# When a paced background step may run: tying the sample-memory sets of a hybrid decoder kernel to the rounds that close a weight group

## The chip, the cores and the metric

The kernel runs on one core of a Trainium2 chip. The metric is the device time of one execution in microseconds. Three executions of the kernel before took 2805.95, 2803.56 and 2801.19 us; their median is 2803.56 us.

## The reference: one step of a two-layer recurrent decoder

The model has 288 tokens: a prompt of 256 and 8 samples of 4 tokens each. Its width is 2048. Layer 0 mixes with a diagonal state space and gated linear attention, layer 1 with an mLSTM of 4 heads of size 512; behind each comes an RMS norm and a squared-ReLU MLP of width 8192. Everything is float32. For this case the mLSTM of layer 1 matters. Each sample brings, for each head, a memory matrix C of 512 x 512 that is both read and updated:

```
num   = (q k^T * w) v + wp * (q C)
den   = sum(q k^T * w) + wp * (q n)
h     = num / max(|den|, exp(-m))
C_new = decay * C + sum_s wk_s k_s v_s^T
```

The 8 samples times 4 heads make 32 matrices of 1 MB, which are loaded, multiplied by the queries, scaled, added to and written back.

## The kernel before, in words

**The stream.** All big products are one stream on TensorE. A `Group` is a weight slice of up to 256 columns; its rows are worked off in *rounds* of 512 rows (four tiles of 128, two column blocks). A round (`mm`, L212) multiplies each of the 8 weight tiles three times against 288 columns, high and low parts of weights and activations (L222, L223, L224), so 24 matmuls. Weights of 2048 rows take 4 rounds, of 1024 rows 2 rounds. The first round of a group *opens* it and takes two PSUM tiles `g` from a pool of two (`psg`, L97); the last *closes* it, and `mm` then emits the evacuations of both tiles (L225 to L228), one VectorE multiplication of 128x288 each: `mq_evac` L1393, `mk_evac` L1396, `mv_evac` L1401, `mo_evac` L1418. While layer 1 runs, `three` is False (L1287), so the next group needs the same two tiles: its opening round waits for the two evacuations.

**Weights.** `load` (L183, SyncE queue) and `cast` (L192) run ahead. A cast makes `wh` on ScalarE (L200) and `wl` on VectorE (L201), two of each per round. The cast that is emitted behind the matmuls of round i is for round i+2.

**The paced steps.** Beside the stream there are generators, kept in `side`. After each round `run` (L230) calls `pump` (L136), with one credit for a full round. Each generator gets its rate times that and makes one step for each whole credit. Steps of `ml_head` (L1423) and `ml_fin` (L1599) have rate 1.0. `ml_mem` (L1546) has rate 0.32 (`R_MEM`, L24), is the only one with `late=1`, and so comes last in the pump. A step may also wait for a flag, and then uses its credit up without work (`until`, L132). `finish` (L153) forces the steps of a generator when a `need` falls due.

**One set of the memories** is one step of `ml_mem`, for two of the eight times 512 KB of a head's samples in a quarter of its rows: 4 matmuls that read the memory into `n` (L1577, two passes each, so x8 in the trace), 4 matmuls of 32 rows that make the new outer products `pb` (L1582, first into the one tile of `psx`, then into three tiles of `pss`, a pool of 3 that every paced step shares), and 4 VectorE operations of 128x512 that scale and add (L1586). After the second and the fourth of them GpSimd's queue issues a store of the tile (L1588) and the load of the tile that comes six half sets later (L1561) into the same buffer; the load waits for the store. There are 8 sets a head, 32 in all. `mem{h}` is set behind the eighth.

**Other paced steps** that the text names: in `ml_head` the scores (L1453), the transposes of k (L1462), a block of small VectorE operations (L1468 to L1481, called the qp block here), the products L1484 and L1492 with a VectorE operation that frees the PSUM tile of the latter (L1494), the denominators with a reciprocal (L1507 to L1514), L1517, four steps with L1528 and four with L1538, whose PSUM tile ScalarE copies out (L1540). In `ml_fin`: L1608, a multiplication of 128x1152 (L1615), squares, and the RMS norm (L1628), which calls `rms` (L288): a square root on ScalarE (L291) and a reciprocal on VectorE (L292).

**Rounds of layer 1** are numbered here from 1, the first of q of head 0. Each of q, k, v and the output gate takes 8 rounds a head, in the order q0 k0 v0, q1 k1 v1, o0, q2 k2 v2, q3 k3 v3, o1, o2, o3; rounds 129 to 160 are the output projection, with a closing round every second one. Up to 128 every fourth closes.

The credits, as the kernel before has them:

```python
for s in sorted(self.side, key=lambda s: s[4]):
    s[2] += s[1] * part
    while s[2] >= 1.0:
        s[2] -= 1.0
        if not self.step(s):
            break
```

Of the kernel before, what the change touches and what calls it, by code (L numbers as in the profile page):

```python
# [21 lines left out]
EPS = 1e-6  # L22
NEG = -1e30
R_S5, R_GLA, R_ML, R_MEM = (1.0, 1.2, 1.15), 1.0, 1.0, 0.32  # L24
R_GST, R_DEC, N_U = 0.5, 0.6, 2


_CONST = {}
# [58 lines left out]
class Base:  # L87
# [45 lines left out]
        while name not in self.flags:  # L133
            yield

    def pump(self, part):  # L136
        for s in sorted(self.side, key=lambda s: s[4]):
            s[2] += s[1] * part
            while s[2] >= 1.0:
                s[2] -= 1.0  # L140
                if not self.step(s):
                    break
# [28 lines left out]
    def flush(self, all_=False):  # L171
        again = True
        while again:
            run, keep = [], []
            for e in self.later:
                e[0] -= 1
                (run if all_ or e[0] <= 0 else keep).append(e)
            self.later = keep
            for e in run:
                e[1]()  # L180
            again = all_ and bool(self.later)
# [48 lines left out]
    def run(self, ahead_load=3, ahead_cast=1):  # L230
        seq = []
        for it in self.items:
            if isinstance(it, Group):
                seq.extend(dict(g=it, k0=k0, n=min(KG, it.nk - k0)) for k0 in it.order)
            else:
                seq.append(it)
        grs = [s for s in seq if isinstance(s, dict)]
        nl = nq = i = 0
        for s in seq:
            if not isinstance(s, dict):  # L240
                s()
                continue
            while nl < min(len(grs), i + ahead_load + 1):
                if nl < len(self.pre):
                    self.pre[nl][0]()
                self.load(grs[nl])
                nl += 1
            while nq < min(len(grs), i + ahead_cast + 1):
                if nq < len(self.pre):
                    self.pre[nq][1]()  # L250
                self.cast(grs[nq])
                nq += 1
            self.mm(s)
            part = 0.5 * s["g"].nm
            s.clear()
            if nq < min(len(grs), i + ahead_cast + 2):
                if nq < len(self.pre):
                    self.pre[nq][1]()
                self.cast(grs[nq])
                nq += 1  # L260
            self.flush()
            self.pump(part)
            i += 1
        self.flush(all_=True)
        self.finish()
# [1000 lines left out]
class Layer1:  # L1266
# [156 lines left out]
    def ml_head(self, h):  # L1423
# [42 lines left out]
        s = self.smp[h] = {}  # L1466
# [42 lines left out]
        nc.tensor.matmul(ps[:, TP:T], lhsT=on[0:32], rhs=w[0:32, 384:416], start=True, stop=False)  # L1509
        nc.tensor.matmul(ps[:, TP:T], lhsT=on, rhs=qn[:, 0, :], start=False, stop=True)  # L1510
        rec = s["rec"] = p.tile([128, T], F32, name="rec", bufs=2)
        act.activation(out=rec, in_=ps, func=AF.Abs)
        v.tensor_max(out=rec, in0=rec, in1=em)
        v.reciprocal(out=rec, in_=rec)  # L1514
# [84 lines left out]
    def ml_fin(self, h):  # L1599
        nc = self.nc  # L1600
        v, act = nc.vector, nc.scalar
        p = self.mlh
        yield from self.until(f"mem{h}")
        yield
        s, hn = self.smp[h], self.hn[h]
        ps = self.pss.tile([128, 4, NS], F32, name="s")
        for e in range(4):
            nc.tensor.matmul(ps[:, e, :], lhsT=s["o"][:, e * 128:e * 128 + 128], rhs=self.c("sel"), start=True, stop=True)  # L1608
        t = p.tile([128, 4, NS], F32, name="inter")
        v.tensor_tensor(out=t, in0=ps, op=ALU.mult,  # L1610
                        in1=s["rec"][:, TP:T].rearrange("p (o t) -> p o t", o=1).to_broadcast([128, 4, NS]))
        v.tensor_add(out=hn[:, :, TP:T], in0=hn[:, :, TP:T], in1=t)
        self.flags.add(f"num{h}")
        yield from self.until(f"so{h}")
        v.tensor_mul(out=hn, in0=hn, in1=self.so[h])  # L1615
        yield
        acc = p.tile([128, T], F32, name="facc")
        for e in range(4):
            if e == 0:
                act.activation(out=acc, in_=hn[:, 0, :], func=AF.Square)  # L1620
            else:
                sq = self.tmp.tile([128, T], F32, name="sq")
                act.activation(out=sq, in_=hn[:, e, :], func=AF.Square)
                v.tensor_add(out=acc, in0=acc, in1=sq)
        yield
        yield
        ps = self.pss.tile([128, T], F32, name="s")
        nc.tensor.matmul(ps, lhsT=self.ones, rhs=acc, start=True, stop=True)  # L1628
        self.rms(acc, ps, 512)
        yield  # L1630
        if h >= 2:
            q, ns = ((self.mlp1, ("q1", "k1")), (p, ("hn", "so")))[h - 2]
            yh, yl = (q.tile([128, 4, T], F32R, name=n, **({} if h == 2 else dict(bufs=2))) for n in ns)
        else:
            yh, yl = (p.tile([128, 4, T], F32R, name=n, bufs=2) for n in ("yh", "yl"))
        self.yy[h] = (yh, yl)
        for e in range(4):
            t = hn[:, e, :]
            v.scalar_tensor_tensor(out=t, in0=t, scalar=self.ml_nw[:, e:e + 1], in1=acc, op0=ALU.mult, op1=ALU.mult)
        yield  # L1640
        for e in (0, 2):
            es = slice(e, e + 2)
            act.activation(out=yh[:, es], in_=hn[:, es], func=AF.Copy)
            self.defer(lambda es=es: v.tensor_tensor(out=yl[:, es], in0=hn[:, es], in1=yh[:, es].bitcast(F32),
                                                     op=ALU.subtract), 0)
            if e == 0:
                yield
        self.flush()
        self.flags.add(f"y{h}")
# [255 lines left out]
```

## Time and profile before

| | before |
|---|---|
| median of 3 executions | 2803.56 us |
| the profiled execution | 2805.46 us |
| its span | 2803.70 us |
| TensorE matmuls busy | 2770.3 us (99%) |
| TensorE weight loads busy | 2679.4 us (96%) |
| VectorE busy | 1704.9 us (61%) |
| ScalarE busy | 1347.2 us (48%) |
| GpSimd busy | 212.5 us (8%) |
| mean granted TensorE clock | 0.996 of full speed |

Layer 1 lies between about 1300 and 1990 us of the span, the memory sets between 1414 and 1882 us. Shares of busy time are averages; a matmul's duration in the trace (about 296 ns for 288 columns) is longer than the distance from one to the next, so TensorE's waits are to be read from starts and from the waits that the profile names. A row of a timeline gives start, duration, engine, line, operation, output<-inputs, shapes and count, and in brackets the idle time before it and what ended it; for x3 the duration covers the three.

### The profile page before, as it was taken

How to read it: one execution, taken by the hardware profiler on the slowest of the kernel's cores; microseconds unless marked ns; L12 is line 12 of the kernel's file. 1: busy time of each engine (PE TensorE's matmuls, PEld its weight loads, DVE VectorE, ACT ScalarE, POOL GpSimd, SP SyncE). 2: the span in 40 equal slices, each digit the busy share in tenths (PEclk: the TensorE clock that was granted, in tenths of full speed). 3: DMA queues.
4: the chain of work that ended last, by engine and by line, in shares of the span. 5: the costliest groups of instructions: out<-in, count | busy, mean ns of one | idle time of the engine just before them, and what ended most of it. 6: DMA issues, size and time to landing. Idle time of an engine off the chain costs nothing. (4 is left out here: it accounts for less than half of the span.)

```text
span 2803.7 us, 52666 instructions
## 1 busy us (share of the span) xinstructions
PE 2770.3 (99%) x20688; PEld 2679.4 (96%) x20688; DVE 1704.9 (61%) x3235; ACT 1347.2 (48%) x2464; POOL 212.5 (8%) x327
## 2 busy tenths in 40 slices
PE   9999999999999999999999999999999999999999
PEld 8988999999999999999988888889999999999999
DVE  7887668555555555557456655777555555555555
ACT  5646755544444444445434343445544444444445
POOL 3110111000000000000112222210000000000000
PEclk9999999999999999999999999999999999999999
DMA  7454567555555555555678878885555555555554
GB/s 212 129 155 140 162 194 227 163 166 166 162 169 165 164 164 165 162 167 150 194 233 262 277 240 277 263 262 160 164 165 165 166 166 166 162 169 161 168 164 136
DMA packets 449737, 511.94 MB, mean 183 GB/s; under 512 B 23315, under 2 KB 423405, under 8 KB 449457
## 3 DMA queue, kind: packets, MB, share of 16 engines
q1 hardware_dynamic: 414320, 412.67, 48.9%
q0 software_dynamic: 28176, 90.22, 10.2%
q10 hardware_dynamic: 6992, 5.68, 0.6%
q8 instruction: 163, 2.67, 0.4%
q14 instruction: 86, 0.70, 0.1%
HBM read 460.15 MB, written 47.56 MB: 181 GB/s over the span
## 5 line engine op out<-in xcount | busy, mean ns | idle before, releaser
L200 ACT ACTIVATE wh<-raw 128x512 fp32r<-128x512 f32 x1556 | 963.1, 629 | 1211.1 <-PE g L223 875.7
L201 DVE TENSOR_TENSOR wl<-raw,wh 128x512 fp32r<-128x512 f32 x1556 | 1036.3, 688 | 663.7 <-ACT wh L200 647.9
L222 PE MATMUL g<-xh,wh 128*128 128x288 f32 x2936 | 885.9, 302 | 6.7 <-DVE so L1418 3.0
L224 PE MATMUL g<-xh,wl 128*128 128x288 f32 x2936 | 867.0, 295 | 3.0 <-DVE wl L201 2.9
L223 PE MATMUL g<-xl,wh 128*128 128x288 f32 x2936 | 869.3, 296 | 0.0
L222 PEld LDWEIGHTS g<-xh,wh 128*128 128x128 f32 x2936 | 553.5, 189 | 22.8 <-issue 12.8
L224 PEld LDWEIGHTS g<-xh,wl 128*128 128x128 f32 x2936 | 555.5, 189 | 4.4 <-DVE wl L201 4.4
L223 PEld LDWEIGHTS g<-xl,wh 128*128 128x128 f32 x2936 | 554.4, 189 | 2.6 <-issue 2.4
L223 PE MATMUL g<-hl,wh 128*128 128x288 f32 x1352 | 400.2, 296 | 0.0
L224 PE MATMUL g<-hh,wl 128*128 128x288 f32 x1352 | 399.5, 296 | 0.0
L222 PE MATMUL g<-hh,wh 128*128 128x288 f32 x1352 | 399.2, 295 | 0.0
L222 PE MATMUL x<-xh,wh 128*128 128x288 f32 x920 | 274.2, 298 | 0.0
L224 PE MATMUL x<-xh,wl 128*128 128x288 f32 x920 | 271.3, 295 | 1.1 <-DVE wl L201 1.1
L223 PE MATMUL x<-xl,wh 128*128 128x288 f32 x920 | 272.0, 296 | 0.0
L222 PEld LDWEIGHTS g<-hh,wh 128*128 128x128 f32 x1352 | 256.9, 190 | 0.0
L224 PEld LDWEIGHTS g<-hh,wl 128*128 128x128 f32 x1352 | 253.5, 188 | 0.0
L223 PEld LDWEIGHTS g<-hl,wh 128*128 128x128 f32 x1352 | 253.3, 187 | 0.0
L223 PE MATMUL x<-hl,wh 128*128 128x288 f32 x696 | 206.0, 296 | 0.0
L224 PE MATMUL x<-hh,wl 128*128 128x288 f32 x696 | 205.7, 296 | 0.0
L222 PE MATMUL x<-hh,wh 128*128 128x288 f32 x696 | 205.5, 295 | 0.0
L224 PEld LDWEIGHTS x<-xh,wl 128*128 128x128 f32 x920 | 173.8, 189 | 1.3 <-DVE wl L201 1.3
L222 PEld LDWEIGHTS x<-xh,wh 128*128 128x128 f32 x920 | 173.1, 188 | 0.9 <-issue 0.8
(567 smaller groups left out, 2949.6 us busy)
## 6 DMA issues: line engine op xcount, KB each, us to landing
raw<-in_w_mlp_up_dram SPq DMA_DIRECT2D x256, 512.0 KB, 3.7
raw<-in_w_mlp_down_dram SPq DMA_DIRECT2D x256, 512.0 KB, 3.6
raw<-in_w_in_odd_dram SPq DMA_DIRECT2D x128, 512.0 KB, 4.6
raw<-in_w_in_even_dram SPq DMA_DIRECT2D x64, 512.0 KB, 4.0
cin<-in_state_mlstm_c_dram POOLq DMA_DIRECT2D x64, 512.0 KB, 5.5
out_sample_mlstm_c_dram<-cin POOLq DMA_DIRECT2D x64, 512.0 KB, 6.0
raw<-in_w_out_even_dram SPq DMA_DIRECT2D x32, 512.0 KB, 4.3
raw<-in_w_out_odd_dram SPq DMA_DIRECT2D x32, 512.0 KB, 3.6
```

What stands on the lines that cost most here:

```text
L200: nc.scalar.activation(out=wh[:, 0:n], in_=src, func=AF.Copy)
L201: nc.vector.tensor_tensor(out=wl[:, 0:n], in0=src, in1=wh[:, 0:n].bitcast(F32), op=ALU.subtract)
L222: nc.tensor.matmul(g.ps[j], lhsT=wh, rhs=xh, start=opens and k == 0, stop=False)
L223: nc.tensor.matmul(g.ps[j], lhsT=wh, rhs=xl, start=False, stop=False)
L224: nc.tensor.matmul(g.ps[j], lhsT=wl, rhs=xh, start=False, stop=closes and k == n - 1)
```

## The change

`pump` gets a second argument, whether the round just done closed its group. A generator with `late` set keeps its credit, without a step, while that credit is under `LATE` = 1.8 and either the round did not close a group or one of three marked steps ran in this pump: the denominators (L1511), the 128x1152 multiplication (L1615) and the RMS norm of a head (L1629). From 1.8 on it steps in any round, once for each whole credit. Nothing else is touched: the same instructions are issued, in another order.

```diff
-R_GST, R_DEC, N_U = 0.5, 0.6, 2
+R_GST, R_DEC, N_U, LATE = 0.5, 0.6, 2, 1.8
...
-    def pump(self, part):
+    def pump(self, part, closes):
+        self.busy = False
         for s in sorted(self.side, key=lambda s: s[4]):
             s[2] += s[1] * part
+            if s[4] and s[2] < LATE and (self.busy or not closes):
+                continue
             while s[2] >= 1.0:
                 s[2] -= 1.0
                 if not self.step(s):
...
-            part = 0.5 * s["g"].nm
+            part, closes = 0.5 * s["g"].nm, s["g"].ps is None
             s.clear()
...
-            self.pump(part)
+            self.pump(part, closes)
...
         rec = s["rec"] = p.tile([128, T], F32, name="rec", bufs=2)
+        self.busy = True
         act.activation(out=rec, in_=ps, func=AF.Abs)
...
         v.tensor_mul(out=hn, in0=hn, in1=self.so[h])
+        self.busy = True
         yield
...
         self.rms(acc, ps, 512)
+        self.busy = True
         yield
```

## Rows read from the trace of the kernel before

**Rows 1.** Busy time by stretch (us, busy and count of each engine, PEclk, DMA, GB/s).
```profile
1200.00:1300.00 100.00, 100.00 (x752) 100.00 (x751) 65.87 (x124) 50.30 (x93) 0.00 (x0) 1.00 0.55 164
1500.00:1600.00 100.00, 97.52 (x694) 82.49 (x694) 66.51 (x107) 40.61 (x70) 25.36 (x40) 1.00 0.87 270
```

**Rows 2.** Waits of TensorE from 1310 to 1900 us: total us, times, longest.
```profile
PE g L222 <- DVE so L1418: 3.0, 2, 1.5
PE s L1582 <- ACT sq L291: 1.2, 1, 1.2
```

**Rows 3.** Timeline of TensorE and VectorE, rounds 63 to 65.
```profile
1574.92 1.07 PE L1577 MATMUL n<-cin,qp 128*32 128x512 f32 x8
1576.35 0.40 PE L222 MATMUL g<-xh,wh 128*128 128x288 f32 x1
1578.22 2.06 DVE L1586 SCALAR_TENSOR_TENSOR cin<-cin,wps,s 128x512 f32<-128x512 f32 x3
1580.20 0.82 DVE L1393 TENSOR_TENSOR q<-g,rbc 128x288 f32<-128x288 f32 x2
1580.79 0.37 PE L222 MATMUL g<-xh,wh 128*128 128x288 f32 x1 [0.98 <-DVE q L1393]
```

**Rows 4.** Timeline of VectorE and TensorE, rounds 51 to 53.
```profile
1516.22 1.95 DVE L1514 RECIPROCAL rec<-rec 128x288 f32<-128x288 f32 x1
...
1521.80 0.40 PE L222 MATMUL g<-xh,wh 128*128 128x288 f32 x1 [1.50 <-DVE so L1418]
```

**Rows 5.** Timeline of TensorE, rounds 125 to 127: L1538 alone, then with a set.
```profile
1847.71 1.88 PE L1538 MATMUL s<-vt,kw 128*128 128x512 f32 x4
1849.02 0.70 PE L222 MATMUL g<-xh,wh 128*128 128x288 f32 x1
...
1852.62 1.88 PE L1538 MATMUL s<-vt,kw 128*128 128x512 f32 x4
1856.20 0.40 PE L222 MATMUL g<-xh,wh 128*128 128x288 f32 x1
```

**Rows 6.** Timeline of TensorE and VectorE, end of round 60.
```profile
1565.13 0.40 PE L222 MATMUL g<-xh,wh 128*128 128x288 f32 x1
1566.24 2.06 DVE L1586 SCALAR_TENSOR_TENSOR cin<-cin,wps,s 128x512 f32<-128x512 f32 x3
```

**Rows 7.** Timeline of TensorE and VectorE, end of round 88.
```profile
1681.97 0.40 PE L222 MATMUL g<-xh,wh 128*128 128x288 f32 x1
1682.55 2.06 DVE L1586 SCALAR_TENSOR_TENSOR cin<-cin,wps,s 128x512 f32<-128x512 f32 x3
```

**Rows 8.** Timeline of TensorE and VectorE, end of round 116.
```profile
1806.53 0.50 PE L1582 MATMUL s<-vs,ks 32*128 32x512 f32 x1 [1.16 <-ACT sq L291]
1806.96 0.40 PE L222 MATMUL g<-xh,wh 128*128 128x288 f32 x1
1809.61 1.40 DVE L1586 SCALAR_TENSOR_TENSOR cin<-cin,wps,s 128x512 f32<-128x512 f32 x2
```

**Rows 9.** Timeline of VectorE and TensorE, rounds 47 and 48.
```profile
1499.70 0.68 DVE L1481 TENSOR_TENSOR hl<-vt,hl 32x512 fp32r<-32x512 f32 x1
1501.15 1.28 DVE L201 TENSOR_TENSOR wl<-raw,wh 128x512 fp32r<-128x512 f32 x2
1502.35 0.34 DVE L1494 SCALAR_TENSOR_TENSOR n<-n,dec,s 128x128 f32<-128x128 f32 x1
1503.22 0.40 PE L222 MATMUL g<-xh,wh 128*128 128x288 f32 x1
```

**Rows 10.** Busy time by stretch, early in layer 1 (columns as in rows 1).
```profile
1329.00:1332.00 3.00, 1.21 (x11) 0.81 (x10) 2.40 (x15) 1.56 (x5) 1.12 (x2) 1.00 0.46 126
1332.00:1335.70 3.70, 3.70 (x17) 3.70 (x18) 1.83 (x8) 0.85 (x2) 0.51 (x2) 0.54 0.83 104
```

**Rows 11.** GpSimd's queue, and the weight loads that waited for a memory tile.
```profile
1861.76 0.71 POOL L1561 DMA_DIRECT2D cin<-in_state_mlstm_c_dram  x1 [7.03 <-DMA out_sample_mlstm_c_dram<-cin]
...
PEld n L1577 <- DMA cin<-in_state_mlstm_c_dram: 1.1, 3, 0.8
```

## The prediction

> **What bounds the kernel now.** I first read busy time by stretch. In a plain stretch TensorE runs without a gap, 752 matmuls in 100 us, so one each 0.133 us and a round of 24 in 3.2 us; in a stretch with memory sets it is still busy for 97.5 of 100 us, VectorE for 66.5 [rows 1]. So TensorE sets the time, and a change of order can only move its waits. Second, TensorE's own waits over the stage of the memories: the largest are two for VectorE before an opening round, 1.5 us each (the output gate's evacuation), and a third of 0.98 us (q's); a further 1.2 us is a wait inside a set for a square root [rows 2, 3]. Third, timelines around these waits, to see what is late and why; last, GpSimd's queue, which feeds the sets.
>
> In the timeline of rounds 63 to 65 a set runs behind round 63, and round 64 closes a group. A set alone holds the stream for 1576.35 - 1574.92 = 1.43 us; its four updates keep VectorE until 1580.28, the two evacuations come behind them, and the opening round 65 starts 0.98 us late [rows 3]. Around round 51 a reciprocal of 1.95 us stands in front of the updates as well, and the wait is 1.50 us [rows 4]; the same happens once more near 1773 us [rows 2].
>
> How good is 97.5% busy as a measure of what can be won? The waits just named, all that have to do with a set, come to 5.2 us. The Trainium skill (Perfetto Trace Analysis, Identifying the Most-Contended Engine) holds that matmul busy time misleads and that the share of weight loading tells the headroom; by it the stretch at 1500 us has 17.5 us in 100 to give, some 80 us over the stage by my estimate. The trace does not agree here: the missing weight loading is time in which matmuls of 512 columns stream behind one small load (the reads of a set [rows 3]). I go by the waits.
>
> **Where the sets go.** Both orders follow from the credits: 0.32 a round from round 17 on, a step for each 1.0, waiting steps counted too. Before, sets run behind rounds 29, 32, 35, 38, 41, 45, 48, 51; 54, 57, 60, 63, 66, 70, 73, 76; 85, 88, 91, 95, 98, 101, 104, 107; 110, 113, 116, 120, 123, 126, 129, 132. With the change I work out: 31, 32, 36, 40, 44, 47, 48, 52; 56, 60, 60, 64, 68, 72, 75, 76; 88, 88, 92, 96, 100, 103, 104, 108; 112, 116, 116, 120, 125, 128, 130, 132. Of 32 sets 27 then stand in a closing round, against 9. But four rounds bring 1.28 credits, more than one set, so the surplus reaches 1.8 five times in another round (31, 47, 75, 103, 125) and reaches 2.0 in three closing rounds (60: 1.76 + 0.32 = 2.08; 88: 2.04; 116: 2.00), where two sets run at once. In 60 and 116 the RMS norm runs too, and the credit overrides the mark. Each head's last set moves by one round at most, and no forced step arises, so the tail of layer 1 stays.
>
> **What is removed.** (1) The 1.5 us wait behind round 51 and its twin behind 107: the sets go to 52 and 108, behind the evacuations in VectorE's order, with three rounds before the next. Minus 3.0 us [rows 2, 4]. (2) The 0.98 us before round 65, as the set of 63 goes to 64: minus 1.0 us [rows 3]. What could be late there next is the weight cast behind the set, but it is due two rounds, 6.4 us, later and the updates take 2.7 us; cost nothing. Without this cover it would cost one cast, 0.64 us [rows 9]. (3) A set in one pump with a product L1538 waits for ScalarE's copy of a PSUM tile: 1856.20 - 1852.62 = 3.58 us, against 1.31 for L1538 alone plus 1.43 for a set, so 0.84 too much [rows 3, 5]. Six sets stand so before (35, 57, 60, 91, 123, 126) and four after (36, the first of 60, 92, 125; the second of 60 is priced below). Two fewer: minus 1.7 us, bounds 0 and minus 1.7.
>
> **What is added.** (4) The two-set rounds. The second set's four products need the four PSUM tiles of the first, so the last of them waits for the first set's last update, and the stream resumes about 0.5 us later (0.43 from the last product to the stream, plus a start [rows 8]). In round 88 the updates end at 1682.55 + 2.06 = 1684.61, the stream resumes at 1685.1 instead of 1681.97 [rows 7]: 3.1 us for 1.43 of work, so 1.7 lost. In round 60 they end at 1568.30, resume at 1568.8 instead of 1565.13 [rows 6]: 3.7 - 1.43 = 2.2 lost. In round 116 the square root already holds the first set for 1.16 us and the reciprocal holds its updates until 1811.01; resume at 1811.5 instead of 1806.96 [rows 8]: 4.55 - 1.43 = 3.1 lost. Together plus 7.0 us; bounds plus 4 (if VectorE gets to the first updates a third earlier) and plus 8. (5) Rounds 47 and 48, twice (103 and 104). The set of 47 stands behind the qp block, which ends at 1500.38. Its four updates (2.7 us) end at 1503.1, then come the evacuations of 48 (0.8), two casts (1.28) and L1494 (0.34), at 1505.5; L1494 frees the PSUM tile that the last product of 48's set needs, so the stream resumes at 1506.0. Without a wait it would at 1503.22 + 1.5 for the set that came in = 1504.7 [rows 9]. So 1.3 us each, plus 2.6; bounds 0 (another free tile) and plus 4. (6) Sets in other pairs (31 with 32, 75 with 76, 125): their updates end before the next closing round's second evacuation is needed, since that round's paced step adds 1 to 3 us of TensorE work. Nothing taken, bounds minus 0.5 and plus 1.5, the size of the wait of [rows 4].
>
> **Queues passed.** Of a moved set its stores and loads on GpSimd's queue move too. There a load waits up to 7.0 us for the store of its buffer [rows 11], two halves a set, some 14 us against 14.6 us between sets on average. So this queue is nearly full, and only the six buffers, three sets of lead, keep the waits for a tile at 1.1 us in three [rows 11]. After the change the tightest place is round 76: its tiles are loaded behind the sets of 60, 60, 64 and 68, four times 14 us behind the first updates at 1566, so by 1622; the set runs 16 rounds behind 1565, 51 us of stream and some 14 of paced steps, near 1630. That leaves 8 us for the load to land. I take nothing; bounds 0 and plus 3. SyncE's weight loads are not passed: they are issued by round, as before.
>
> **The sum.** -3.0 - 1.0 - 1.7 + 7.0 + 2.6 = +3.9 us. The profiled execution took 2805.46 us (span 2803.70 and 1.76 around it), so it would take 2809.4; it lies 1.9 above the median of the three, 2803.56, and against that the forecast is 2807.5 us. That is 0.14%, under the 0.2% (5.6 us) that a measurement of this kernel can tell from no change.
>
> **Rivals.** *The clock falls in the two-set rounds* (slower). Early in layer 1 TensorE did 1.2 us of work in 3 us, waiting for gates, and the next 3.7 us ran at a granted clock of 0.54, the level of 1.2 GHz: 17 matmuls where 28 fit, 1.5 us lost [rows 10]. In round 116 after the change the engine waits for about 4 us with little between. If the clock falls behind all three, it is 3.9 + 3 x 1.5 = 8.4: 2812 us. Against it: the stretch at 1500 us holds a wait of 1.50 and one of 0.98 us at a granted clock of 1.00 [rows 1, 3, 4]. [...]
>
> *The bunched sets drain the buffers* (slower): the second set of a pair waits for its tiles, from the point where the 8 us are used up; half of a load's wait of 7.0 us more [rows 11], 2811 us. For it speaks the queue that is nearly full, against it the lead.
>
> *The second set's waits lie beside work that the stream had to wait for anyway* (faster): then terms 4 and 5 fall to nothing and the removed waits stay, -5.7: 2797.9 us. The waits of [rows 2] speak for it; against it stands the pool of three PSUM tiles.
>
> *The change doesn't do what it says*: if the surplus credit broke the rule most of the time, nothing would move and it would stay at 2803.6; counting gives 27 of 32, so I give it no chance of its own.
>
> **How the numbers follow.** The sum's case has 0.60, the clock 0.14, the buffers 0.11, the faster rival 0.15. The sum's own bounds (-5.7 + 4 + 0 to -4 + 8 + 4) reach from about 2802 to 2812; of its 0.60 I put 0.12 above 5.6 us. The clock and the buffers lie above it whole. The faster rival lies on the edge, so half of it counts. So slower 0.37, faster 0.08, same 0.55. The range of 2799.5 to 2812.5 takes in the sum's bounds, the buffers, the clock at two of three places (2810.5) and the weaker half of the faster rival.
>
> **What would show it.** Right: the waits of q and the output gate on VectorE gone from TensorE's list; in their place waits of L1582 on VectorE's updates (or their PSUM tiles) in rounds 60, 88 and 116 of 2 to 4 us, and on L1494 in 48 and 104 of 1.3 us; granted clock 1.00 in these rounds. Wrong: a second set that follows the first at 1.43 us; waits of L1577 on a load; a stretch at 0.5 of the clock; or new waits before opening rounds.

## The result, and the profile after

The changed kernel is slower by 0.7%: 2825.31 us, median of 6 runs (2818.97 to 2828.17), against 2803.24 (2801.19 to 2807.06, 6 runs) for the kernel before beside it. The ratio is 1.0074 [1.0063, 1.0085]. The forecast was 2807.5 with a range up to 2812.5.

| | before | after |
|---|---|---|
| profiled execution, us | 2805.46 | 2828.17 |
| its span, us | 2803.70 | 2826.40 |
| granted clock, mean | 0.996 | 0.991 |
| matmuls | 20688 | 20688 |

**By stretch.** Lines below the diff have moved by 3 to 6: L222 is now L225, L1538 L1542, L1540 L1544, L1582 L1586, L1586 L1590. The first view is busy time by stretch, with the columns of [rows 1]; its second line answers to the second of [rows 1].

```profile
1400.00:1500.00 100.00, 96.54 (x653) 84.04 (x656) 51.10 (x84) 33.53 (x60) 16.41 (x25) 0.97 0.73 219
1500.00:1600.00 100.00, 97.47 (x656) 81.50 (x649) 64.52 (x106) 39.30 (x69) 22.47 (x34) 0.97 0.79 244
1700.00:1800.00 100.00, 95.95 (x676) 82.90 (x675) 55.71 (x94) 38.70 (x70) 25.38 (x40) 0.97 0.84 255
1800.00:1900.00 100.00, 97.62 (x650) 81.98 (x648) 68.31 (x110) 44.27 (x75) 19.13 (x27) 0.97 0.82 272
```

In the stretch at 1500 us TensorE's busy share is what it was (97.47 against 97.52), yet 656 matmuls ran instead of 694, and the granted clock is 0.97 instead of 1.00. Busy time hides this loss: at half the clock matmuls start 0.24 us apart instead of 0.133, and the engine counts as busy all the same. The two half-clock stretches in this window (at 1528 and 1576 us, below) account for some 22 of the 38 missing matmuls by my estimate; waits, and the other rounds that the window holds, make up the rest.

**TensorE's waits**, 1300 to 1930 us: engine, tile and line that waits, what it waits for; total us, times, longest. They answer to [rows 2].

```profile
PE s L1586 <- ACT cp L1544: 5.9, 3, 3.5
PE s L1586 <- ACT vs L1522: 2.6, 2, 1.3
PE x L1586 <- DVE cin L1590: 1.4, 2, 1.1
PE g L225 <- DVE hr L1713: 1.3, 2, 1.1
PE s L1586 <- ACT sq L294: 1.2, 1, 1.2
PE s L1586 <- DVE n L1497: 0.8, 2, 0.4
```

The waits for `so` (3.0 us) are gone, and so is the one for q. The two largest now are waits of a set's products L1586 for ScalarE: for `cp`, the copy of L1542's result, which the forecast had at 0.84 us a place and shrinking, and for `vs`, which it hadn't at all.

**The clock.** Busy time around three of the places where it fell, and around two where it didn't, round 7 (the place of [rows 10]) and round 88; columns as above.

```profile
1328.00:1331.00 3.00, 1.19 (x11) 0.79 (x10) 2.40 (x15) 1.58 (x5) 1.14 (x3) 1.00 0.48 125
1331.00:1334.70 3.70, 3.70 (x29) 3.70 (x30) 2.18 (x9) 1.28 (x3) 0.49 (x1) 1.00 0.75 109
...
1446.00:1453.50 7.50, 4.04 (x18) 1.22 (x16) 3.72 (x6) 1.57 (x3) 0.70 (x1) 0.94 0.77 240
1453.50:1457.50 4.00, 4.00 (x17) 4.00 (x18) 1.13 (x2) 0.63 (x1) 3.19 (x7) 0.50 0.81 258
...
1523.00:1527.20 4.20, 2.90 (x18) 1.08 (x17) 4.03 (x8) 3.75 (x6) 1.45 (x2) 1.00 0.64 189
1527.20:1531.00 3.80, 3.80 (x18) 3.80 (x19) 2.21 (x4) 0.63 (x1) 0.72 (x2) 0.56 0.96 273
...
1687.00:1693.50 6.50, 6.17 (x38) 2.96 (x36) 5.27 (x9) 0.63 (x1) 0.76 (x1) 1.00 0.46 140
1693.50:1697.00 3.50, 3.50 (x26) 3.44 (x26) 2.81 (x5) 0.81 (x2) 1.43 (x2) 1.00 0.43 129
...
1819.00:1828.00 9.00, 6.78 (x33) 2.75 (x32) 6.70 (x9) 3.08 (x5) 2.71 (x4) 0.81 0.85 270
1828.00:1832.00 4.00, 4.00 (x18) 3.77 (x18) 2.10 (x5) 0.63 (x1) 0.12 (x1) 0.57 0.86 262
```

Behind round 36 (TensorE busy for 4.04 of 7.50 us) the next 4 us hold 17 matmuls at 0.50, the level of 1.2 GHz, where 30 fit, as in [rows 10]. Behind round 52 (2.90 of 4.20 us busy) and round 116 (6.78 of 9.00) it fell as well. In round 88 the engine was busy for 6.17 of 6.50 us and the clock held. Round 7 isn't touched by the change: with the same work, 11 matmuls in 3 us, the clock fell behind it in the profile before (17 matmuls in 3.7 us) and held in the profile after (29). So the same wait costs the clock in one execution and not in another.

**The whole difference, in two sums.** In the timeline of TensorE a round's last stream matmul and the next round's first stand 0.133 us apart where nothing lies between. What lies there beyond 0.133 is the end of a round: the set, the paced step, and their waits. From 1290 to 1940 us, the stage of the memories, the ends add up to 143.92 us before and 160.17 after: plus 16.25. Inside the rounds, matmuls start 0.24 us apart at half the clock instead of 0.133; that costs 1.49 us before, in the one place of [rows 10], and 9.67 after, in six places (2.46 at 1454 us, 1.50 at 1528, 1.46 at 1576, 1.50 at 1719, 1.49 at 1791, 1.26 at 1829): plus 8.2. The wait of q before round 65, behind a round without a step, took 1.14 us from start to start and is gone. Together 16.25 + 8.2 - 1.1 = +23.3 us; the spans differ by 22.7, and layer 1 begins 1.0 us earlier in the profile after.

Ends of the rounds that differ by more than the place of a plain set, us (* a set, ** two; plain L1542 is 1.31, a plain set 1.43 to 1.53):

| round | before | after | | round | before | after |
|---|---|---|---|---|---|---|
| 35, 36 | 3.44*, 1.32 | 1.32, **7.48*** | | 91, 92 | 3.47*, 1.31 | 1.32, **6.06*** |
| 48 | 2.88* | 3.83* | | 104 | 2.89* | 3.83* |
| 51, 52 | 2.85*, 2.09 | 1.32, **3.75*** | | 107, 108 | 2.85*, 2.09 | 1.32, **3.74*** |
| 57, 60 | 3.25*, 3.88* | 1.32, **7.52**** | | 116 | 3.66* | **8.48**** |
| 76 | 1.96* | 2.82* | | 123, 125, 126 | 3.25*, 1.31, 3.59* | 1.31, **3.89***, 1.31 |
| 88 | 2.70* | **5.81**** | | | | |

### The profile page after: what moved, and what is told of

The parts are those of the page before. It is cut to its first block, busy times and chain, and to the rows that moved or that the text cites. A ratio compares the mean times of both kernels' runs of the same rounds, so it can differ in the third digit from the quotient of the medians.

```text
span 2826.4 us, 52666 instructions
## 1 busy us (share of the span) xinstructions
PE 2786.4 (99%) x20688; PEld 2691.1 (95%) x20688; DVE 1705.5 (60%) x3235; ACT 1346.6 (48%) x2464; POOL 212.5 (8%) x327
## 5 line engine op out<-in xcount | busy, mean ns | idle before, releaser
L225 PE MATMUL g<-xh,wh 128*128 128x288 f32 x2936 | 889.6, 303 | 2.7 <-DVE gy L971 1.4
L225 PEld LDWEIGHTS g<-xh,wh 128*128 128x128 f32 x2936 | 556.9, 190 | 17.8 <-issue 12.4
L225 PE MATMUL g<-hh,wh 128*128 128x288 f32 x1352 | 399.2, 295 | 0.0
L225 PE MATMUL x<-xh,wh 128*128 128x288 f32 x920 | 274.2, 298 | 0.0
L225 PEld LDWEIGHTS g<-hh,wh 128*128 128x128 f32 x1352 | 256.9, 190 | 0.0
L225 PE MATMUL x<-hh,wh 128*128 128x288 f32 x696 | 205.5, 295 | 0.0
L225 PEld LDWEIGHTS x<-xh,wh 128*128 128x128 f32 x920 | 173.0, 188 | 0.9 <-issue 0.8
```

What stands on the lines that cost most here:

```text
L225: nc.tensor.matmul(g.ps[j], lhsT=wh, rhs=xh, start=opens and k == 0, stop=False)
```

## The experiments

My theory after the two traces (L): sets wait for PSUM tiles that other work frees late, the copy of L1542's result and the copy L1518 (now L1522) above all, the two-set rounds add theirs, and the clock falls behind these waits. Its rivals: the clock alone is the loss, so that mending one wait only moves the fall; or GpSimd's queue (Q), which can't follow the bunched sets, holds them whatever else is mended. L+Q is both.

Each kernel ran beside the kernel before, whose medians on the three occasions were 2804.15 (15 runs; 1 to 3), 2806.29 (17; `a_fill`, `n_busy`, `a_all`, `n_busy_fix`) and 2804.20 (19; the rest). Times of different occasions are compared by their ratios to it; 0.001 is 2.8 us.

**1 to 3: one suspect at a time.** First round 36 in the kernel after: timeline of TensorE and ScalarE, start and duration in us, then in brackets the idle time before and what ended it.

```profile
1445.36 0.34 ACTq L1545 DMA_DIRECT2D out_prompt_mlstm_c_dram<-cp  x1
1445.93 1.88 PE L1542 MATMUL s<-vt,kw 128*128 128x512 f32 x4
1447.74 1.06 PE L1581 MATMUL n<-cin,qp 128*32 128x512 f32 x8
1452.04 0.60 ACT L1544 ACTIVATE cp<-s 128x512 f32<-128x512 f32 x1 [5.07 <-DMA out_prompt_mlstm_c_dram<-cp]
1452.69 0.79 PE L1586 MATMUL s<-vs,ks 32*128 32x512 f32 x1 [3.46 <-ACT cp L1544]
```

L1542's result was ready near 1447.8. The copy to `cp` started at 1452.04, because `cp` has one buffer and the store of the copy before, issued at 1445.36, had not landed. The copy frees the PSUM tile that the set's last product needs. Copies fall behind at L1542 after L1542: behind rounds 33 to 36 the first waited only for its product, the next three for a store, for 1.83, 3.02 and 5.07 us. Round 36 has the head's fourth.

Then round 52, the same view; it answers to [rows 4]:

```profile
1523.41 0.50 PE L1521 MATMUL s<-hl,rsel 64*128 64x512 f32 x1
1524.04 1.28 ACT L1422 ACT_TABLE_LOAD   x1
1525.33 0.78 ACT L1422 ACTIVATE so<-so 128x288 f32<-128x288 f32 x2
1526.01 0.58 ACT L1522 ACTIVATE vs<-s 128x512 fp32r<-128x512 f32 x1
1526.64 0.50 PE L1586 MATMUL s<-vs,ks 32*128 32x512 f32 x1 [1.30 <-ACT vs L1522]
```

The sigmoids' table load, 1.28 us, stands ahead of the copy L1522 on ScalarE, and the set waits for the PSUM tile that this copy frees.

`a_cp2`, two buffers for the copy (the second in the room of a tile that another one can share):

```diff
-            cp = p.tile([128, 512], F32, name="cp")
+            cp = p.tile([128, 512], F32, name="cp", bufs=2)
...
-        t = p.tile([128, 4, NS], F32, name="inter")
+        t = p.tile([128, 4, NS], F32, name="qn")
```

> The changed kernel with two buffers for the copy of the L1538 product (its small inter tile shares a buffer with qn to make room). Theory L (late tiles): a set that shares a pump with another paced step waits for a PSUM tile that ScalarE or VectorE frees late, and a TensorE kept this thin falls to half clock for a while. In rounds 36 and 92 the copy waits for the store of the copy before. With two buffers the ends of rounds 36 and 92 take 2.7 to 3.5 us instead of 7.5 and 6.1, and the stretches at half clock behind them (2.5 and 1.5 us lost) are gone: 10 to 12 us less than the changed kernel, 2813 to 2815 us. Rival Q (queue): the stores and loads of the sets on GpSimd's queue set the pace now, as their share of the chain of waits suggests; then no tile of ScalarE matters and it stays at 2825 (2822 to 2828).

Measured: 2817.92 us (2813.40 to 2822.93), 1.0052 [1.0037, 1.0066]. Some 6 us less than the kernel after by the ratios, where 10 to 12 were expected. Round 36 fell from 7.48 to 3.25 us, 92 from 6.06 to 3.24, and the clock held behind both. But round 76 grew from 2.82 to 5.73. In the kernel after, this round's last memory tile was already late: the weight load that needs it waited 0.73 us, until 1637.63. Now the round was 7.9 us earlier and the tile only 5.0, so the wait grew to 3.63 us, until 1632.60. The weight loads' waits for memory tiles in that profile:

```profile
PEld n L1581 <- DMA cin<-in_state_mlstm_c_dram: 4.4, 2, 3.6
```

So the copy was the cause of 36 and 92, and behind it stood the rival of the drained buffers, in part. `b_cp2`, the same edit to the kernel before, is the control:

> Control: the kernel before with the same two buffers for the copy. It has no set beside the fourth L1538 of a head but six beside an earlier one, 0.8 us too long at most. Theory L: 0 to 4 us less than before, 2799 to 2803, and no other granted clock. Rival Q: no change, 2803. If it gained as much as the change loses (10 us or more), the copy's buffer would be a bound of its own and not one that the change brings.

Measured: 2802.25 us (11 runs), 0.9991 [0.9982, 1.0000]. The buffer wins next to nothing where no set stands behind four products L1542 in a row.

`a_so2`, the sigmoids one round later:

```diff
-            self.defer(lambda: nc.scalar.activation(out=t, in_=t, func=AF.Sigmoid))
+            self.defer(lambda: nc.scalar.activation(out=t, in_=t, func=AF.Sigmoid), 2)
```

> The changed kernel with the sigmoids of the output gate put off by one more round, so that they and their table load no longer stand ahead of the copy that frees L1521's PSUM tile in rounds 52 and 108. Theory L: the ends of these rounds take about 2.0 us instead of 3.75 and the half clock behind them (1.5 us each) is gone: 6 to 7 us less, 2818 to 2820 us. Rival Q: no change, 2822 to 2828.

Measured: 2824.32 us (2819.95 to 2826.25), 1.0076 [1.0062, 1.0089]. In its profile, rounds 52 and 108 fell from 3.75 to 1.96 us and the clock holds behind them, as expected; it fell at 1452, 1687 and 1818 us instead. The mechanism is confirmed in the two rounds; the gain of 6 to 7 us is not seen in the times. The profile can't say where it went: it is of the fastest of the five executions (2819.95 us), 8.2 us shorter than that of the kernel after, with ends of rounds that add up to 4.6 us less. In the other four executions the granted clock was 0.991 or 0.992, as low as in most of the kernel after, so the clock's part of the gain didn't come; what took the rest stays open, and the intervals leave room for some 4 us.

`a_one`, one set at a time:

```diff
-                if not self.step(s):
+                if not self.step(s) or s[4]:
                     break
```

> The changed kernel with at most one set a pump: the second sets of rounds 60, 88 and 116 run behind 63, 91 and 119. Theory L: the ends of the three rounds go from 7.5, 5.8 and 8.5 us to about 3.9, 2.7 and 3.7, the sets cost 1.4 to 2.2 us where they go to, and the half clock behind 60 and 116 (1.5 and 1.3 us) is gone: 7 to 10 us less, 2815 to 2818 us. Rival Q: the same number of sets in the same time through the same queue, no change, 2822 to 2828.

Measured: 2816.77 us (2811.93 to 2823.22), 1.0049 [1.0033, 1.0065], as expected. The surplus sets went to rounds 63, 91 and 119, at ends of 1.53, 3.31 and 3.86 us.

**4: the clock by itself.** `a_fill` adds 113 matmuls on the stream's own tiles, whose result nothing uses, between the reads and the products of the sets that waited. Nothing that a set waits for comes sooner by them; they only keep TensorE at work meanwhile.

```diff
+                fill = {(0, 2): 26, (2, 2): 17, (0, 7): 10, (2, 7): 10, (1, 2): 14, (2, 1): 14, (3, 1): 8, (3, 2): 14}
+                for _ in range(fill.get((h, n), 0)):
+                    nc.tensor.matmul(pb[0][:, 0:T], lhsT=self.xh[:, 0, 0:128], rhs=self.xh[:, 0, :], start=True, stop=True)
```

> The changed kernel with useless matmuls (128x288, into the tile that the first product of the set overwrites) in the places where a set waits: 26 in round 36, 17 in 92, 10 each in 52 and 108, 14 each in the second sets of 60, 88 and 116, 8 in the first of 116; 113 in all, 15 us of TensorE work at 0.133 us each. Theory C (clock): the six stretches at half clock of the changed kernel's profile (9.7 us lost) come from TensorE standing nearly still in these waits. Filled, the waits are as long as before and the granted clock stays at 1.00: 5 to 9 us less than the changed kernel, 2816 to 2820 us. Rival W (waits alone): the clock has another cause; the filler gains nothing and costs what doesn't fit into the waits, 2825 to 2835 us.

Measured: 2821.79 us (2821.05 to 2823.51), 1.0052 [1.0040, 1.0065]: by the ratios some 6 us less than the kernel after (1.0074 [1.0063, 1.0085]), though the intervals just touch, with 113 x 0.133 = 15 us more matmul work. That is within the 5 to 9 us of theory C; its 2816 to 2820 us are missed only because the kernel before took 3 us longer on this occasion. Busy time around rounds 36, 60 and behind 116 in its profile, the copy of round 36, and TensorE in round 60 (L1586 is the filler here, L1589 the products):

```profile
1445.00:1452.80 7.80, 7.80 (x48) 5.21 (x47) 2.57 (x5) 1.23 (x2) 0.70 (x1) 1.00 0.82 263
1452.80:1457.00 4.20, 4.20 (x34) 4.20 (x33) 3.11 (x5) 1.26 (x2) 3.56 (x7) 1.00 0.77 241
1560.00:1574.00 14.00, 11.76 (x54) 6.57 (x52) 6.41 (x9) 4.13 (x6) 2.83 (x4) 0.77 0.61 191
1828.00:1832.00 4.00, 4.00 (x33) 4.00 (x32) 3.01 (x6) 2.42 (x4) 0.62 (x1) 1.00 0.92 341
```
```profile
1451.00 0.60 ACT L1544 ACTIVATE cp<-s 128x512 f32<-128x512 f32 x1 [5.37 <-DMA out_prompt_mlstm_c_dram<-cp]
...
1567.64 0.79 PE L1589 MATMUL s<-vs,ks 32*128 32x512 f32 x1 [2.12 <-ACT cp L1544]
1568.35 1.94 PE L1581 MATMUL n<-cin,qp 128*32 128x512 f32 x8
1570.22 3.73 PE L1586 MATMUL x<-xh 128*128 128x288 f32 x14
```

The copy waits for its store as before (5.37 us), yet the stream behind round 36 runs at 1.00, 34 matmuls in 4.2 us, and in the stage of the memories no stretch of the stream is at half clock. Only in round 60 did the clock fall, and there the filler bears the theory out in its own way: it stood only before the second set's products, but in this execution the first set waited 2.12 us for ScalarE's copy with nothing to fill it. Behind that wait the second set's eight reads took 1.94 us instead of 1.06 and the 14 fillers 3.73 instead of 1.9, and the round grew to 13.38 us. So the ends of the rounds take 4.5 us more than in the kernel after, and the stream between them gives back 9.9. The half clock is thus a consequence of the thin waits, and its cost is apart from theirs. The executions agree: their mean granted clock is 0.995 to 0.996, against 0.991 to 0.994 for the kernel after, and they lie within 2.5 us against 9.2.

**5: which part of the rule.** `n_busy` keeps the marks and drops the closing round; `c_only` does the reverse.

```diff
-            if s[4] and s[2] < LATE and (self.busy or not closes):
+            if s[4] and s[2] < LATE and self.busy:
```

> Half of the change alone: a set avoids only the rounds with a marked step (until 1.8 credits), whether they close a group or not. The sets of 51, 57, 60, 107, 113 and 116 move one round back, all others stay. Theory L: the wait of 2 us in round 116 and of 0.6 us in 60 go, rounds 52 and 108 keep 1.8 us of wait (now for the copy behind the table load): 2 us less than before, plus 0 to 3 us of half clock: 2801 to 2805 us, no measurable difference. If the marks and not the closing rounds made the change slow, it would be near 2825.

Measured: 2805.88 us (11 runs), 1.0002 [0.9993, 1.0012]: no difference, as expected, but not by the terms expected. In its profile (2812.28 us, one of the two longest executions) the ends of the rounds take 4.1 us more than before. The set that the marks move to round 58 stands beside L1542 with a late copy there and costs 6.01 us, those of 91 and 126 cost 5.18 and 4.77. With two buffers (`n_busy_fix`, below) the three cost 3.30, 3.24 and 3.24.

```diff
-            if s[4] and s[2] < LATE and (self.busy or not closes):
+            if s[4] and s[2] < LATE and not closes:
```

> The other half of the change alone: sets wait for closing rounds (until 1.8 credits), the marks of long steps are not looked at. The order differs from the changed kernel in one set only (behind 124 instead of 125, beside the RMS norm and L1538). Theory L: as the changed kernel or 0 to 3 us more, 2823 to 2829 us; all of the loss is the closing rounds'. If the marks bore part of it: nearer to before, below 2818.

Measured: 2824.18 us (2821.72 to 2828.69), 1.0073 [1.0059, 1.0086]. The loss belongs to the closing rounds whole; the marks change nothing that can be measured in the time.

**6: all mends together, and the queue.** `a_all` has the three edits of 1 to 3.

> The changed kernel with the three repairs together: two buffers for the copy, sigmoids put off, one set a pump. Theory L: taken from the three traces, the ends of all rounds together take 143 to 147 us instead of 160, as in the kernel before (144), with 0 to 4 us of half clock: 2801 to 2808 us, no measurable difference from before. If waits for the memory tiles in rounds 76 and 119 grow (3.6 and 2 us where they were seen), the upper end. Rival (something else in the change costs): it stays at 2812 us or more.

Measured: 2822.59 us (2814.12 to 2825.47), 1.0050 [1.0036, 1.0063]: 14 us above the upper end. The waits for `cp` and `vs` are gone; TensorE's and its weight loads' waits, and GpSimd's, show what came:

```profile
PE n L1581 <- DMA cin<-in_state_mlstm_c_dram: 8.4, 3, 6.5
PE s L1586 <- DVE w L1459: 3.3, 1, 3.3
PEld n L1581 <- DMA cin<-in_state_mlstm_c_dram: 12.7, 5, 7.4
...
POOL cin L1565 <- DMA out_sample_mlstm_c_dram<-cin: 339.8, 58, 8.5
POOL out_sample_mlstm_c_dram L1592 <- DVE cin L1590: 46.4, 5, 26.6
```

The ends of the rounds still add up to 160.93 us; rounds 75, 120 and 132 now take 9.66, 5.30 and 10.20. GpSimd issues a load right behind the store of the same buffer and stands for 339.8 us waiting for these stores, and the stores and loads behind it stand with it. The 3.3 us on L1459, in round 75, hang on this queue too: the operand `bc` of VectorE's work there is a load that GpSimd issues, and VectorE waited 6.68 us for it. In the kernel after it is 305.2 us in 58 waits, the longest 7.9; before, 303.3 in 58, the longest the one of [rows 11]. So the queue stood nearly as long before; that the evenly spread sets left it enough time is my reading of it. `a_all_q` is `a_all` with each load issued one store later, into the buffer whose store was issued earlier:

```diff
-        for g in range(CB):
+        for g in range(CB - 1):
...
-                        load(g + b // 2 + CB)
+                        load(g + b // 2 + CB - 1)
```

> The changed kernel with the three repairs and a freed queue: each load of a memory tile is issued one store later, so that GpSimd's queue no longer stands still until the store just issued has landed. With the repairs alone the waits for late PSUM tiles were gone, but in their profile waits for memory tiles took 12.7 us (rounds 75, 120 and 132). Theory L+Q: the closing rounds bunch the sets on a queue that is nearly full, and this is what came in place of the late tiles; with the queue freed the ends of all rounds take 143 to 147 us and it is 2800 to 2808 us, no measurable difference from before. Theory L alone, with another cause for those waits (the memory itself or the DMA engines): they stay, 2815 to 2825 us.

Measured: 2798.51 us (12 runs, 2797.14 to 2801.99), 0.9980 [0.9972, 0.9988], some 20 us less than `a_all` by the ratios and a little below the range of L+Q. The waits for memory tiles are gone, the ends add up to 142.45 us, the half clock costs 1.64, all of it in round 7. GpSimd's waits:

```profile
POOL cin L1565 <- DMA out_sample_mlstm_c_dram<-cin: 77.2, 32, 4.0
POOL out_sample_mlstm_c_dram L1592 <- DVE cin L1590: 262.7, 28, 31.0
```

It now waits for the updates, as a queue with time to spare does. `a_q` has this edit alone, on the kernel after:

> The changed kernel with the freed queue alone. Theory L+Q: its own profile has 1.7 us of waits for memory tiles, so the queue isn't what it waits for as it stands; 0 to 3 us less, 2822 to 2826 us. Rival Q: the queue is the cause, and it falls by 10 us or more, below 2815.

Measured: 2817.48 us (2813.25 to 2821.82), 1.0047 [1.0033, 1.0060], between the two cases. It does not separate them: the freed queue also let the stores of `cp` land sooner (median 4.0 us from issue against 4.8), so round 36 fell to 4.45 without a second buffer.

**7: the better kernel.** The rule that cost the time is left out, the marks and the mends of `cp` and the sigmoids stay (`n_busy_fix`); then the freed queue as well (`n_fix_q`).

> The same half with the two repairs that don't belong to the order: two buffers for the copy and the sigmoids put off. Theory L: further 3.6 us in rounds 52 and 108 and about 1.4 us beside L1538: 6 to 7 us less than before, 2796 to 2799 us, and faster than both kernels. If the waits removed come back elsewhere: 2801 to 2805.

Measured: 2796.85 us (2795.66 to 2799.51), 0.9964 [0.9953, 0.9976]. The ends add up to 137.48 us, 6.4 less than before.

> The half with the marks and its two repairs, with the freed queue. Its profile has 1.1 us of waits for memory tiles in five places. Theory L+Q: no measurable difference from it, 0.9955 to 0.998 of the kernel before, 2794 to 2799 us. If the queue held back more than the waits show: 5 us less than without it or more.

Measured: 2796.00 us (2794.67 to 2798.15, 8 runs), 0.9968 [0.9956, 0.9979]. Not to be told from `n_busy_fix`; both beat the kernel before by over 0.2%. Waits of TensorE of over 0.5 us from 1300 to 1930 us in `n_fix_q`, then the copy's waits on ScalarE there:

```profile
PE g L225 <- DVE hr L1713: 1.3, 2, 1.1
PE s L1384 <- ACT fe L1365: 1.1, 1, 1.1
PE g L225 <- DVE q L1396: 1.0, 1, 1.0
```
```profile
ACT cp L1544 <- PE s L1542: 13.4, 12, 1.2
```

No set waits for 0.5 us or more, and no copy for a store; in the kernel after the copies waited for 23.0 us on stores.

## Why the prediction was wrong

| step | predicted, us | measured, us |
|---|---|---|
| (1) rounds 51 and 107 | -3.0 | +0.3 |
| (2) q's wait before round 65 | -1.0 | -1.1 |
| (3) sets beside L1538 | -1.7 | +5.9 |
| (4) two-set rounds | +7.0 | +7.3 |
| (5) rounds 47/48 and 103/104 | +2.6 | +1.9 |
| queue, round 76 | 0 (to +3) | +0.9 |
| the clock (rival: 4.5) | 0 | +8.2 |
| sum | +3.9 | +23.3 |

The column on the right is from one profile of each kernel, as worked out above, and rounded; the 8.2 is the 9.7 us behind the six places less the 1.5 of round 7 before.

**Where the sets go** was right in every round. **(2), (4) and (5)** were right as mechanisms and nearly as sizes: the two-set rounds 60, 88 and 116 took 7.52, 5.81 and 8.48 us. The timeline of TensorE shows it, for rounds 48, 60 and 116 [rows 9, 6, 8]:

```profile
1507.96 0.49 PE L1586 MATMUL s<-vs,ks 32*128 32x512 f32 x1 [0.42 <-DVE n L1497]
...
1571.71 0.50 PE L1586 MATMUL x<-vs,ks 32*128 32x512 f32 x1 [0.32 <-DVE cin L1590]
1572.37 0.49 PE L1586 MATMUL s<-vs,ks 32*128 32x512 f32 x1 [0.16 <-DVE cin L1590]
1573.03 0.50 PE L1586 MATMUL s<-vs,ks 32*128 32x512 f32 x1 [0.17 <-DVE cin L1590]
1573.68 0.50 PE L1586 MATMUL s<-vs,ks 32*128 32x512 f32 x1 [0.16 <-DVE cin L1590]
...
1822.98 0.49 PE L1586 MATMUL s<-vs,ks 32*128 32x512 f32 x1 [1.16 <-ACT sq L294]
1825.53 0.79 PE L1586 MATMUL x<-vs,ks 32*128 32x512 f32 x1 [1.06 <-DVE cin L1590]
```

In round 60 the second set's products follow the first set's updates one by one, 0.66 us apart; in 116 the square root holds the first set for the same 1.16 us as before, and the second waits behind the reciprocal and the updates; in 48 the last product waits for L1497, as forecast, but 0.42 us and not the 1.3.

**(3) failed by 7.6 us, the most of the five terms.** "Six sets stand so before and four after" took the 0.84 us of [rows 5] as the price of any set beside L1538. That price is not one of the pair: it is how late the chain copy, store, next copy is by then. Of the five places before with nothing else beside (35, 57, 91, 123, 126), the cheapest cost 0.51 and the dearest 0.85 over 1.31 + 1.43; rounds 36 and 92 stand at a head's fourth L1538 and cost 4.74 and 3.32. The store of `cp` is an issue on ScalarE's queue with its own landing time (median 4.8 us), against L1538 every 4.91 us in rounds 33 to 36. `a_cp2` shows it: with two buffers both fall to 3.25 us. The bounds "0 and minus 1.7" had no row for the fourth.

**(1) failed in "behind the evacuations in VectorE's order".** That order was right, and the waits it meant are gone. But a set needs a PSUM tile too, and in 52 and 108 the tile is freed by ScalarE's copy L1518 behind the table load and the sigmoids of the same evacuations. A wait of 1.30 us on another engine took the place of the 1.50. `a_so2` shows this in both rounds.

**The clock was taken as nothing, and this step is 8.2 us off.** As a rival it stood at three places of 1.5 us and a chance of 0.14; it fell at six, at two of those three (60 and 116) and at 36, 52, 92 and 108. The argument against it was that the stretch at 1500 us before holds waits of 1.50 and 0.98 us at 1.00 [rows 1]. Those are single waits with a busy stream on both sides; the new ones lie inside a set or between two, whose products leave gaps of their own (TensorE busy for 4.04 of 7.50, 2.90 of 4.20 and 6.78 of 9.00 us in rounds 36, 52 and 116). The places priced were also only those of term 4, while the waits that came with terms 1 and 3 drew the clock down as well. The granted clock was 0.50 to 0.57 behind these three rounds, and 1.00 behind 36 and 116 when filler kept the array at work. The Trainium skill (TensorE: Matmul & The Clock Gate, What's actually happening) says that the clock is throttled by default and that activity releases it; these granted clocks agree with that. What stays open is why one wait costs the clock and the next like it doesn't: round 7 lost it before and kept it after, the six executions of the kernel after have a mean clock from 0.991 (2828.17 us) to 0.994 (2818.97), and in the profiles round 88 [rows 7] kept the clock in the kernel after and lost it at 1687 us in `a_so2`, with the same waits of 0.16 to 0.17 us between the same products.

**The drained buffers** (0.11, at 2811 us) had the right queue and the right round, 76, but as a rival alone it was small: +0.9 us. It decided only when other waits were taken away (`a_all`). The 8 us of lead were not there: the round's last load was issued at 1632.06 us, not by 1622, and the round's stream ended at 1636.1, not near 1630. So 4 us were left for a load that took 5.5. That it cost only 0.9 us hangs on a stream that was late itself; in `a_cp2`, with the stream 7.9 us earlier, it cost 3.8.

## What to carry to other kernels

Before a step is moved next to another, follow every buffer that both of them touch, PSUM tiles and staging tiles with their stores included, to the engine that frees it, and price the place by how far that chain is behind there; one row of the same pair elsewhere prices only that place. A wait with thin work around it on TensorE can have two prices, itself and the half clock behind it, and the second is seen in matmuls per stretch, not in busy time. When several waits are mended and the time doesn't move, look for the queue that was hidden behind them.

## What the runs showed of the hardware

- Useless matmuls in a wait paid for themselves: 113 of them took the half-clock stretches out of the stream in the stage of the memories (9.67 us in the profile of the kernel after) and lowered the ratio from 1.0074 to 1.0052 (`a_fill`).
- Much of the spread between executions of the kernel after goes with the clock: 9.2 us from end to end with a mean clock of 0.991 to 0.994, where 0.001 of 2826 us is 2.8 us, so 8.5 us by estimate.
- Issuing GpSimd's loads one store later, with one buffer less in flight, cut its waits for stores from 339.8 us to 77.2 and was worth 1.0050 - 0.9980 = 0.0070, some 20 us, once the other waits were mended (`a_all` against `a_all_q`), and nothing that can be measured where the sets stay spread out (`n_busy_fix` against `n_fix_q`).
